# Softmax denominators of a hybrid encoder layer: laid out by VectorE and DRAM in place of TensorE and on-chip transfers

## The chip, the cores and the metric

The kernel runs on one core of a Trainium2 chip. A core has a matrix engine (TensorE, PE in the profile), a vector engine (VectorE, DVE), a scalar engine (ScalarE, ACT), a general engine (GpSimd, POOL) and a queue engine (SyncE, SP). Each works through its own list of instructions in order and waits at semaphores for the others. Transfers are issued from the SP and POOL queues and are carried out by 16 DMA engines. The metric is the device time of one execution in microseconds (us); lower is better. Three runs of the kernel before gave 528.19 to 529.47 us, median 529.1 us.

## What is computed

One layer of an encoder over 512 positions of width 1024, in float32: RMSNorm, one input projection, a recurrent group (a convolution and two linear scans) beside an attention group, an output projection, and a feed-forward part of width 4096 with a last RMSNorm. The change lies in the attention group, which has eight heads of width 64:

```
logits = einsum('bqhd,bqjhd->bhqj', qb, kg) * scale + bias          # per dilated window
lse    = logsumexp(logits);  p = exp(logits - lse)
o      = sum over the three windows of softmax(lse) * (p @ v)
```

The three windows with their softmax over `lse` are the same as one softmax over all keys, in which a key that lies in several windows counts several times. The kernel computes it so: exponentials e of all keys (the log of the multiplicity is in the bias), their row sum z for each query and head, and y = (e @ v) / z. The row sums are produced with one value per partition, because the queries lie on the partitions there. The product e @ v is produced transposed, with the 64 values of a head on the partitions and the 512 queries along the row, so 1/z has to be turned from a column into a row and repeated on 64 partitions. That turning is what is changed.

## The kernel before

Matrix products are done as three passes on numbers split into a high and a low part (`mm3`, lines 311 to 314). The weights come in blocks of 128x1024 into a ring of three buffers (`wraw`) by `emit_dma` (L230), are split by ACT (`conv_hi`, L247) and DVE (`conv_lo`, L269), and are used by PE some steps later.

The attention is worked in pairs of heads, p = 0 to 3, in a loop over i = 0 to 4 and u = 0 to 3 (lines 1142 to 1177). PE, ACT, DVE, POOL and, inside this loop, SP execute in the order in which the code writes their instructions out. A step (i, u) holds:

- `att_s(i, u)`: scores of pair i for one block of 128 queries, four matmuls (L797) into two PSUM banks. The tag `gs` has two banks, so the scores of the next step need that both banks were read.
- `att_t`: for pair i-1, transposes of the exponentials on PE (L838), copied out of PSUM by ACT (L843). `att_c` turns remaining 32-column pieces on DVE (L851).
- `att_e(i, u)`: DVE adds the bias tile `tw` to the scores and takes the row's least value (L813), ACT takes the exponential and its row sum (L814). The sums of a pair are eight columns in `zs[p]`.
- at u = 0, `att_z(i-1)`: the reciprocal of the eight sums (L868), and a copy that repeats each 16 times (L870), 128x128 in `z16`.
- `att_t` of the second head at u = 1 also transposes `z16` on PE (L840), and ACT copies the result back (L845). Row 32*qt + 16*e + w then holds the 128 values of query block qt and head e of the pair.
- at u = 1, `att_zd(i-1)`: four transfers on SP's queue (L877) copy each group of 32 rows, each row four times, into 128 partitions of `zrow`.
- `att_av`: the products e @ v (L941), of pair 0 at i = 2, of pairs 1 and 2 at i = 4, of pair 3 behind the loop. Each ends with `yp` = product * `zrow` on DVE (L947). From `yp` follow the squares for the attention's norm (`ysq`, L594 and L600), their column sums on PE (`turned`, L430, at 180.50 us) and the scaled `at` (L961).
- between them fillers: projections of the later pairs (`pqk`) and of the output (`pwo`), whose PSUM banks are emptied by DVE (L985), with `x` loaded by SP (L1049) in the same step as the weight sums `ws` (L1052).

The bias tiles `tw` are read from DRAM by pairs of SP transfers (L466, L468), at u = 2 for the first half and at u = 0 for the second half of a pair's query blocks. Each SP transfer also waits for the completion of the transfer issued eight before it, because there are eight completion semaphores in turn.

## Time and profile before

| what | us |
|---|---|
| median of three runs | 529.1 (528.19 to 529.47) |
| the profiled execution, its own time | 528.82 |
| its span, first to last instruction | 527.0 |
| PE busy | 520.1 |
| DVE busy | 433.7 |
| ACT busy | 357.1 |
| POOL busy | 65.8 |
| attention loop, first scores to the last product's `yp` | 95.3 to 177.8 |

The profile names a line of the program, its engine, output <- input, and a count. In a list of pieces in order of time the first number is the start from the span's start, the second the duration. In a row of a transfer the duration is that of the issue on the queue; the time from issue to landing stands apart. The 'DMA share' of a stretch is the mean busy share of the 16 DMA engines; values over 1 arise where packets of two queues overlap on an engine.

### The profile page before, as it was taken

The page shows a single profiled execution, that of the slowest core. Times are in us where ns is not written, and L with a number is a line of the kernel's source. Part 1 is how long each engine was busy: PE and PEld are TensorE (multiplying, and loading weights), DVE is VectorE, ACT ScalarE, POOL GpSimd, SP SyncE. Part 2 cuts the span into 40 slices and gives each one's busy share as a digit, 9 for nine tenths or more (in the row PEclk, how much of TensorE's full clock was granted, in tenths as well). Part 3 has the DMA queues.
Part 4 walks back from the last instruction along what each step waited for, and adds up shares of the span by engine and source line. Part 5 has one row for each costly group of instructions (what it writes and reads, how often), then busy time and mean ns, then how long its engine had stood idle before and what let it go on. Part 6 is the DMA issues. An engine that isn't in the chain of part 4 may idle for free.

```text
span 527.0 us, 8246 instructions
## 1 busy us (share of the span) xinstructions
PE 520.1 (99%) x3001; PEld 448.8 (85%) x3001; DVE 433.7 (82%) x665; ACT 357.1 (68%) x578; POOL 65.8 (12%) x88
## 2 busy tenths in 40 slices
PE   9999999999999999999999999999999999999995
PEld 8856888887887788899999888888999999888884
DVE  5898788997877888898779987889756987987885
ACT  6578983788856757585577755576467677655664
POOL 0184000000000131001300311001101200131000
PEclk9999999999999999999999999999999999999999
DMA  7646446596696498947495899976978497799704
GB/s 285 213 133 162 151 140 189 149 249 190 134 317 208 136 189 230 340 158 203 115 224 142 219 270 274 311 283 160 279 224 217 107 224 214 160 297 265 174 1 159
DMA packets 42441, 106.64 MB, mean 202 GB/s; under 512 B 4865, under 2 KB 15233, under 8 KB 42401
## 3 DMA queue, kind: packets, MB, share of 16 engines
q1 hardware_dynamic: 34848, 80.14, 45.9%
q0 software_dynamic: 7408, 25.79, 26.4%
q8 instruction: 23, 0.38, 0.3%
q10 hardware_dynamic: 144, 0.20, 0.1%
q14 instruction: 18, 0.14, 0.1%
HBM read 94.54 MB, written 4.23 MB: 187 GB/s over the span
## 4 chain that ended last, share of the span: by engine, by line
PE 98%; DVE 0%; issue 0%; DVEq 0%; ACT 0%; ACTq 0%
PE pu L313 10%; PE pu L312 10%; PE pu L314 10%; PE pd L312 10%; PE pd L314 10%; PE pd L313 10%; PE pqk L312 3%; PE pqk L314 3%; PE pqk L313 3%; PE pwo L312 3%; PE pwo L314 3%; PE pwo L313 3%; PE ps L797 2%; PE pav L941 2%; PE pt L838 2%; PE pv L312 2%
## 5 line engine op out<-in xcount | busy, mean ns | idle before, releaser
L269 DVE TENSOR_TENSOR wlo<-wraw,whi 128x1024 fp32r<-128x1024 f32 x71 | 86.6, 1220 | 23.8 <-ACT whi L247 23.5
L247 ACT ACTIVATE whi<-wraw 128x1024 fp32r<-128x1024 f32 x67 | 70.9, 1059 | 32.1 <-PE pd L314 20.2
L313 PE MATMUL pd<-wlo,ah 128*128 128x512 f32 (+1 forms) x195 | 75.2, 386 | 0.0
L312 PE MATMUL pd<-whi,ah 128*128 128x512 f32 (+1 forms) x195 | 75.2, 386 | 0.0
L314 PE MATMUL pd<-whi,al 128*128 128x512 f32 (+1 forms) x195 | 75.2, 386 | 0.0
L247 ACT ACTIVATE whi<-tw 128x1024 fp32r<-128x1024 f32 x38 | 40.2, 1060 | 40.5 <-DMA tw<-in_w_up_dram 12.2
L313 PE MATMUL pu<-hl,whi 128*128 128x256 f32 x224 | 63.4, 283 | 0.0
L314 PE MATMUL pu<-hh,wlo 128*128 128x256 f32 x224 | 63.4, 283 | 0.0
L312 PE MATMUL pu<-hh,whi 128*128 128x256 f32 x224 | 63.4, 283 | 0.0
L269 DVE TENSOR_TENSOR wlo<-tw,whi 128x1024 fp32r<-128x1024 f32 x38 | 46.4, 1220 | 18.6 <-ACT whi L247 18.6
L312 PE MATMUL pu<-h2h,whi 128*128 128x256 f32 (+1 forms) x200 | 60.1, 300 | 0.0
L314 PE MATMUL pu<-h2h,wlo 128*128 128x256 f32 (+1 forms) x200 | 60.0, 300 | 0.0
L313 PE MATMUL pu<-h2l,whi 128*128 128x256 f32 (+1 forms) x200 | 60.0, 300 | 0.0
L312 PEld LDWEIGHTS pu<-hh,whi 128*128 128x128 f32 x224 | 43.0, 192 | 0.0
L313 PEld LDWEIGHTS pu<-hl,whi 128*128 128x128 f32 x224 | 43.0, 192 | 0.0
L314 PEld LDWEIGHTS pu<-hh,wlo 128*128 128x128 f32 x224 | 43.0, 192 | 0.0
L314 PEld LDWEIGHTS pd<-whi,al 128*128 128x128 f32 x195 | 36.6, 188 | 7.4
L313 PEld LDWEIGHTS pd<-wlo,ah 128*128 128x128 f32 x195 | 36.6, 188 | 7.4
L312 PEld LDWEIGHTS pd<-whi,ah 128*128 128x128 f32 x195 | 36.6, 188 | 7.2
L247 ACT ACTIVATE whi<-ts 128x1024 fp32r<-128x1024 f32 x24 | 25.5, 1061 | 24.4 <-PE pd L314 18.1
L312 PEld LDWEIGHTS pu<-h2h,whi 128*128 128x128 f32 x200 | 38.3, 191 | 1.3
L314 PEld LDWEIGHTS pu<-h2h,wlo 128*128 128x128 f32 x200 | 38.3, 191 | 1.3
(276 smaller groups left out, 1246.0 us busy)
## 6 DMA issues: line engine op xcount, KB each, us to landing
wraw<-in_w_up_dram SPq DMA_DIRECT2D x25, 512.0 KB, 4.3
ts<-in_w_dn_dram POOLq DMA_DIRECT2D x24, 512.0 KB, 13.7
wraw<-in_w_dn_dram SPq DMA_DIRECT2D x24, 512.0 KB, 9.1
tw<-in_w_up_dram SPq DMA_DIRECT2D x15, 512.0 KB, 6.7
tw<-in_w_up_dram POOLq DMA_DIRECT2D x15, 512.0 KB, 8.3
wraw<-in_w_in_dram SPq DMA_DIRECT2D x13, 512.0 KB, 3.7
ts<-in_w_dn_dram SPq DMA_DIRECT2D x8, 512.0 KB, 7.1
tw<-in_w_dn_dram SPq DMA_DIRECT2D x8, 512.0 KB, 6.6
```

The lines of the kernel that those rows point to most:

```text
L247: act(hi, raws[i], AF.Copy)
L269: nc.vector.tensor_tensor(lo, r, f(splits[i][0]), op=OP.subtract)
L312: nc.tensor.matmul(o, lhsT=a[0], rhs=b[0], start=bool(first), stop=False, skip_group_check=on)
L313: nc.tensor.matmul(o, lhsT=a[0], rhs=b[1], start=False, stop=False, skip_group_check=on)
L314: nc.tensor.matmul(o, lhsT=a[1], rhs=b[0], start=False, stop=bool(last), skip_group_check=on)
L797: nc.tensor.matmul(psq[p][e][:, :NK], lhsT=sp[p, 0, n, e][:, c0:c0 + P], rhs=k, start=i == 0, stop=i == 1)
L838: nc.tensor.transpose(pt[:, i * P:(i + 1) * P], en[h][qt][:, k:k + P], ident)
L941: nc.tensor.matmul(pav[p][a, co], lhsT=vs[:, jt, h * DH:(h + 1) * DH], rhs=et[h, jt][:, ci], start=jt == 0 and i == 0, stop=jt == 3 and i ...
```

## The change

- The eight sums are ordered by head and then query block (column 4*e + qt in place of 2*qt + e).
- `att_z` writes their reciprocals into the first eight columns of a 128x32 tile that was zeroed once at the start (`rz32`, one more memset on POOL), and turns the tile on DVE in squares of 32x32 into `zt`. One transfer writes `zt` to a DRAM tile `zd`: all 32 rows of each square, 128 pieces of 32 values. It is issued by SP where `att_z` stands, at u = 0.
- `att_zd` reads `zrow` from there in one transfer: two rows of 512 values, each repeated on 64 partitions. It stands at u = 2 in place of u = 1, except for the last pair, where it stays at u = 1.
- Gone are the copy to 128x128, the PE transpose, ACT's copy out of PSUM, and the four transfers.

```diff
+    rz32 = consts.tile([P, 32], FT, name="rz32")
     nc.gpsimd.memset(mhalf, -0.5)
+    nc.gpsimd.memset(rz32, 0.0)
...
-            act(x, x, AF.Exp, scale=-1.0, bias=mn, accum_out=zs[p][:, 2 * qt + e:2 * qt + e + 1])
+            act(x, x, AF.Exp, scale=-1.0, bias=mn, accum_out=zs[p][:, 4 * e + qt:4 * e + qt + 1])
...
-        z = z16[h // 2] if (h % 2, jt) == (0, 1) else None
...
-        if z is not None:
-            nc.tensor.transpose(pt[:, 3 * P:], z, ident)
...
-        if z is not None:
-            act(z, pt[:, 3 * P:], AF.Copy)
...
+    zd = dram.tile([4, 32, P], FT, name="zd")
+
     def att_z(p):
-        rz = small("rz", 8)
-        nc.vector.reciprocal(rz, zs.pop(p))
-        z16[p] = g_("z16")[:, :P]
-        nc.vector.tensor_copy(z16[p], fan(rz, 0, 8, 16))
+        nc.vector.reciprocal(rz32[:, :8], zs.pop(p))
+        zt = work.tile([P, 32], FT, name="zt", tag="zt", bufs=2)
+        nc.vector.transpose(zt, rz32)
+        nc.sync.dma_start(bass.AP(tensor=zd.tensor, offset=zd.offset + 32 * P * p, ap=[[32, 4], [P, 32], [1, 32]]), zt)
 
     def att_zd(p):
         zrow[p] = g_("zrow")
-        t = z16.pop(p)
-        for qt in range(4):
-            r = t[32 * qt:32 * qt + 32]
-            nc.sync.dma_start(zrow[p][:, qt * P:(qt + 1) * P],
-                              bass.AP(tensor=r.tensor, offset=r.offset, ap=[r.ap[0], [0, 4], [1, P]]))
+        nc.sync.dma_start(zrow[p], bass.AP(tensor=zd.tensor, offset=zd.offset + 32 * P * p, ap=[[S, 2], [0, DH], [1, S]]))
...
-                if u == 1 and i >= 1:
+                if u == (1 if i == 4 else 2) and i >= 1:
                     att_zd(i - 1)
```

More of the change, by code (lines that the diff above doesn't have):

```diff
@@ L828, in blocks @@
         return (own + oth, slice(0, NK)) if hj else (oth + own, slice(S - NK, S))
-    z16 = {}
     def att_t(h, jt):
```

## The prediction

> **What bounds the kernel now.** I read the page's busy times first, then the chain that ended last, then PE's waits.

> ```profile
> span 527.0 us, 8246 instructions
> ...
> PE 520.1 (99%) x3001; PEld 448.8 (85%) x3001; DVE 433.7 (82%) x665; ACT 357.1 (68%) x578; POOL 65.8 (12%) x88
> ...
> PE 98%; DVE 0%; issue 0%; DVEq 0%; ACT 0%; ACTq 0%
> ```
> ```profile
> PE pwarm L142 <- PEq L1800: 0.8, 1, 0.8
> ```

> PE is busy in 99% of the span and makes 98% of the chain; its only recorded wait is 0.8 us before the first matmul. So an instruction taken from DVE, ACT, POOL or SP is worth nothing by itself, one taken from PE is worth its own time, and every new wait of PE is paid in full, because PE has no idle time in which to make it up. What can happen is therefore a small certain gain, and a loss where the new path to `zrow` makes something late that PE uses.

> How near to late things are is seen where the change lies. The chain in order of time, then DVE's list in order of time:

> ```profile
> 150.69 0.33 PE pt L838 x3
> 151.02 0.11 PE pt L840
> 151.13 0.33 PE pt L838 x3
> ...
> 153.53 0.56 PE ps L797 x3
> ```
> ```profile
> 130.46 0.69 DVE L947 TENSOR_TENSOR yp<-pav,zrow 128x512 f32<-128x512 f32 x1 [0.42 <-PE pav L941]
> ...
> 149.94 0.75 DVE L985 SCALAR_TENSOR_TENSOR x<-pwo,rcol,x 128x512 f32<-128x512 f32 x1 [0.71 <-DMA x<-in_xn_dram]
> ...
> 151.74 0.58 DVE L813 CUSTOM_DVE_ANT_0 e<-ps,tw 128x416 f32<-128x416 f32 x1
> ...
> 164.46 0.16 DVE L868 RECIPROCAL rz<-zz 128x8 f32<-128x8 f32 x1
> 164.65 0.23 DVE L870 COPY z<-rz 128x128 f32<-128x128 f32 x1
> ...
> 167.71 0.69 DVE L947 TENSOR_TENSOR yp<-pav,zrow 128x512 f32<-128x512 f32 x1 [2.14 <-PE pav L941]
> ...
> 177.10 0.69 DVE L947 TENSOR_TENSOR yp<-pav,zrow 128x512 f32<-128x512 f32 x1
> ...
> 179.42 0.69 DVE L600 TENSOR_TENSOR ysq<-ysq 128x512 f32<-128x512 f32 x1
> ```
> ```profile
> 180.50 0.60 PE L430 MATMUL pcs<-ident,ysq 128*128 128x128 f32 x4
> ```

> Two places are tight. At 149.94 DVE has already waited 0.71 us for a load of `x`; behind it stand the two L813 that empty the score banks, the first done at 151.74 + 0.58 = 152.32, and PE writes into that bank at 153.53: 1.2 us of slack. And the last pair's `yp` at 177.10 leads over `ysq`, done at 179.42 + 0.69 = 180.11, to PE's column sums at 180.50: 0.4 us.

> **What goes and what comes on the engines.** PE loses four transposes L840, 0.11 us each on the chain: -0.44 us, the one sure term. ACT loses four copies out of PSUM and DVE exchanges its copy for a turn of 128x32, whose nearest row is L851, the same operation on the same shape:

> ```profile
> L845 ACT ACTIVATE z<-pt x4: 263/270/273, 115.5 to 169.4; 128x128 f32<-128x128 f32 x4
> ```
> ```profile
> L851 DVE STREAM_TRANSPOSE ett<-e x32: 167/186/208, 111.6 to 173.5; 128x32 f32<-128x32 f32 x32
> ```

> 4 x 0.27 us of ACT and 4 x (0.23 - 0.19) us of DVE are saved, beside PE: counted as nothing. The order of the sums in `zs` costs nothing. The added memset on POOL stands behind one of 0.10 us and ahead of a wait for the first load:

> ```profile
> 1.25 0.10 POOL L136 MEMSET mhalf<- 128x4 f32 x1
> 3.56 0.19 POOL L337 COPY ag<-tw 128x8 f32<-128x8 f32 x1 [2.21 <-DMA tw<-in_xw_dram]
> ```

> Between nothing and twice that row's time (32 columns in place of 4), an estimate, it vanishes in those 2.21 us of waiting; without that wait it would delay the first matmuls by as much.

> **What goes and comes on SP's queue.** Sixteen transfers of 64 KB become four writes of 16 KB and four reads of 256 KB.

> ```profile
> L877 SPq DMA_DIRECT2D zrow<-z x16: 550/598/1107, 117.5 to 171.9; - x16
> ...
> DMA to landing us min/median/max: 2.1/2.1/6.6
> ```
> ```profile
> 122.26 0.43 SPq L468 DMA_DIRECT2D tw<-nbd  x1
> ...
> 137.48 2.54 SPq L877 DMA_DIRECT2D zrow<-z  x4
> 140.06 0.59 SPq L466 DMA_DIRECT2D tw<-nbd  x1
> ...
> 142.23 0.41 SPq L1052 DMA_DIRECT2D ws<-in_w_out_dram  x1
> 142.74 2.08 SPq L1049 DMA_DIRECT2D x<-in_xn_dram  x2
> ...
> 159.35 0.43 SPq L230 DMA_DIRECT2D wraw<-in_w_up_dram  x1
> ```

> Issue time falls, from four times 0.6 us to twice 0.6 us per pair. The write waits for DVE's turn (for the last pair 164.65 + 0.19 = 164.84) and holds what is queued behind it: for pairs 0 to 2 the q transfers or loads of `x`, by no more than its own 0.6 us, because the turn is done when SP comes there; for pair 3, where it comes last, the first block of `w_up`, issued at 159.35 before, which goes to 165.5. ACT first touches that block at 194.13, so 6 us later is covered; if it weren't, ACT's split of it and PE's use would move with it.

> ```profile
> 194.13 1.05 ACT L247 ACTIVATE whi<-wraw 128x1024 fp32r<-128x1024 f32 x1
> ```

> POOL's transfers keep their place. The write's landing is needed by the read alone. For pairs 0 to 2 the bias tiles stand between them; for pair 3 only that block, so SP waits there for the landing, with later weight blocks behind it, which are as early as that first one.

> **The unknown: how long the read holds its DMA engines.** The read names two rows and repeats each 64 times. The least leading count in any transfer of the trace is 32, so how a count of 2 is dealt out is shown nowhere. The bounds come from the rate of one engine and from two loads of the same 256 KB, one plain, one that repeats a row on 128 partitions:

> ```profile
> q1 hardware_dynamic: 34848, 80.14, 45.9%
> ```
> ```profile
> L1049 SPq DMA_DIRECT2D x<-in_xn_dram x8: 328/334/1656, 142.7 to 159.0; - x8
> ...
> DMA to landing us min/median/max: 3.5/5.3/7.4
> ```
> ```profile
> L1719 SPq DMA_DIRECT2D fgt<-in_fg_dram x2: 481/640/798, 466.8 to 469.8; - x2
> ...
> DMA to landing us min/median/max: 10.0/12.0/14.0
> ```

> 80.14 MB in 45.9% of 16 x 527 us is 20.7 KB per us and engine. Spread on 16 engines the 262 KB hold each for 0.8 us, as the four old transfers did; on two for 6.3 us, 5.5 us more. One engine alone, 12.7 us, is the far end. The repeating load lands 12.0 - 5.3 = 6.7 us later than the plain one at the median. The value nearest to that is 5.5 us, and I take two engines; the queue was full around `fgt` too, so this is a choice and not a proof.

> [...]

> **What lies behind the read.** A transfer has its share on every engine, so what follows on the queue waits for those two.

> ```profile
> 137.50:145.00 7.50, 7.50 (x42) 6.55 (x41) 6.12 (x18) 6.78 (x17) 0.00 (x0) 1.00 0.61 119
> 145.00:165.00 20.00, 20.00 (x119) 16.23 (x119) 16.24 (x42) 12.58 (x33) 0.00 (x0) 1.00 0.97 316
> 165.00:167.50 2.50, 2.50 (x24) 1.41 (x20) 0.57 (x1) 1.24 (x2) 0.00 (x0) 1.00 0.49 195
> 167.50:172.50 5.00, 5.00 (x34) 4.27 (x32) 4.39 (x11) 3.11 (x9) 0.00 (x0) 1.00 0.15 35
> ```

> The last two columns are DMA share and GB/s.

> Pair 0's read stands behind the bias load that was issued at 122.26, so it is issued by 122.7 at the latest; at 2.1 + 5.5 us it lands by 130.3, and its `yp` starts at 130.46 because the products end then: hidden, though barely (each us of lateness would first use up DVE's 0.42 us of idle time). Pair 1's read stands ahead of `ws` and `x`. The engines are idle for 0.39 x 7.5 = 2.9 us in 137.5 to 145, which takes up that much; 5.5 - 2.9 = 2.6 us remain. `x` then comes at 152.5 in place of 149.94, the first L813 ends at 154.9, and PE, which arrives at 153.53 - 0.33 = 153.2, waits 1.7 us.

> Pair 2's read falls where the share is 0.97, so nothing takes it up. Its own `yp` comes at 167.71 and is safe, but both reads together, 11.0 - 2.9 - 0.6 = 7.5 us, push the end of the backlog from 165 + 0.49 x 2.5 = 166.2 to 173.7. The last pair's write, issued at 165, lands at the end of that backlog, and only then may the read start: 173.7 + 2.1 (least landing of `zrow`) + 5.5 = 181.3. `yp` would have come at 177.10 + 1.7 - 0.44 = 178.4; it is 2.9 us late, of which 0.4 are slack: PE waits 2.5 us at L430. Sum: -0.44 + 1.7 + 2.5 = +3.8 us.

> With one engine at the 316 GB/s and 0.97 of the full stretch (20.4 KB per us) this is unchanged; if a lone pair of engines is a tenth faster, the read adds 5.0 us, the two waits are 1.2 and 1.5 us, and the sum is +2.3 us. I take +3.0 us between them. On the profiled execution's 528.82 us that is 531.8; the median of the runs is 0.3 us above it, so I forecast 532.1.

> **The rivals.**
> (a) Not slower: the read is spread widely. From four engines up it holds them 3.2 us, 2.4 more than before, less than the 2.9 us gap, and both places stay covered. Then only the transposes go: 528.7. For it: every transfer in the trace runs on many engines, SP's issue time falls, and the DMA share of 0.15 after 167.5 leaves the last pair 5 us. Against it: the landing of `fgt`.
> (b) The last read lands like `fgt`: 12.0 us after an issue at 173.2, at 185.2, against 178.1: 7.1 - 0.4 = 6.7 us at L430, with 1.5 at L797 and -0.44 in all +7.8: 536.9. Against it: the queue is emptier there.
> (c) Two engines, but the waits shorter than 1 us each, because the loads behind are issued ahead of need: 529.1 to 530.7. Against it: DVE's 0.71 us at L985, already a wait for such a load.

> **Chances and range.** The measurement tells 0.3%, 1.6 us, from no change. Two engines with more than that: 0.50; like `fgt`: 0.10; (c) 0.08; (a) 0.29; faster by over 0.3%, for which no row gives a mechanism beyond 0.44 us, 0.03. Slower 0.60, same 0.37, faster 0.03. The likeliest case alone lies between 530.7 and 535; the range takes in (a) below, with the run to run spread, and (b) above: 528.4 to 537.

> **What the new profile would show.** The transposes: no L840, PE's busy time down 0.44. The read: landing of `zrow` at 7 us or more against 2 to 5 if it is spread. Stage by stage: an L985 that waits for `x` over 0.71 us near 150, PE waits on DVE at L797 near 153; `yp` of the last pair waiting on `zrow` and PE on L600 at L430. If PE still has no wait, (a) holds and the forecast is wrong. It is wrong as well if the lateness shows at loads that I took as covered, such as the bias tiles.

## The result, and the profile after

The changed kernel takes 536.04 us (535.63 to 536.71) where the kernel before takes 529.17 us (528.19 to 529.47): the ratio is 1.0134, 95% interval 1.0116 to 1.0152. It is slower, by 6.9 us. The profiled execution took 535.63 us.

The page after: span, busy times and, last, the chain that ended last by engine.

```profile
span 533.9 us, 8221 instructions
...
PE 521.4 (98%) x2997; PEld 448.5 (84%) x2997; DVE 433.5 (81%) x665; ACT 356.0 (67%) x574; POOL 65.8 (12%) x89
...
PE 86%; DMA 9%; DVE 2%; ACT 1%; issue 1%; SPq 0%; DVEq 0%; ACTq 0%
```

PE has four matmuls fewer, yet the span is 6.9 us longer. Before, 98% of the chain was PE; now 9% of it is DMA. PE's waits (total, times, longest) were one of 0.8 us; now there are three more, all behind DVE:

```profile
PE ps L799 <- DVE mn L815: 2.6, 1, 2.6
PE pcs L432 <- DVE ysq L602: 1.5, 1, 1.5
PE pt L837 <- DVE cs L437: 1.2, 1, 1.2
PE pwarm L144 <- PEq L1793: 0.8, 1, 0.8
```

DVE's own list in order of time shows what it waited for: pair 0's `zrow` near 132, the loads of `x` near 154 and the last pair's `zrow` near 184. (L940 was L947, L978 was L985, L799 was L797, L837 was L838, L432 was L430.)

```profile
132.10 0.69 DVE L940 TENSOR_TENSOR yp<-pav,zrow 128x512 f32<-128x512 f32 x1 [2.73 <-DMA zrow<-zd]
...
154.21 0.75 DVE L978 SCALAR_TENSOR_TENSOR x<-pwo,rcol,x 128x512 f32<-128x512 f32 x1 [5.07 <-DMA x<-in_xn_dram]
...
184.12 0.69 DVE L940 TENSOR_TENSOR yp<-pav,zrow 128x512 f32<-128x512 f32 x1 [2.08 <-DMA zrow<-zd]
```

The last `yp` is at 184.12 where it was at 177.10: 7.0 us later, of which 0.4 us were slack. The chain in order of time shows the way there: pair 3's write takes 5.0 us to land, and its read 9.0 us.

```profile
170.02 4.96 DMA zd<-zt
174.98 0.02 SPq L871
175.05 8.98 DMA zrow<-zd
```

And there is a loss that no list of waits shows. Behind the longest wait the granted clock (third column from the right) falls to half; the last two columns are DMA share and GB/s (the share of 1.01 is queue q1's alone, 101.4%, so a value over 1 needs no second queue):

```profile
157.50:160.00 2.50, 2.50 (x11) 2.18 (x10) 2.10 (x4) 1.64 (x5) 0.00 (x0) 0.50 0.88 152
160.00:162.50 2.50, 2.50 (x11) 2.08 (x10) 1.64 (x5) 1.19 (x4) 0.00 (x0) 0.83 1.01 390
```
```profile
156.65 0.45 PE L799 MATMUL ps<-kk,qh 128*128 128x416 f32 x1 [2.59 <-DVE mn L815]
...
161.99 0.35 PE L799 MATMUL ps<-kk,qh 128*128 128x416 f32 x1
```

From these scores to the next ones PE needs 161.99 - 156.65 = 5.34 us. In the kernel before the same work ran from 153.37 to 156.85:

```profile
153.37 0.35 PE L797 MATMUL ps<-kk,qh 128*128 128x416 f32 x1
...
156.85 0.35 PE L797 MATMUL ps<-kk,qh 128*128 128x416 f32 x1
```

That is 3.48 us, so 1.9 us are lost there. In this execution the loss adds up along PE as 1.2 + 2.6 + 1.9 + 1.5 - 0.4 (the transposes) = 6.8 us of the 6.9 us of span.

### The profile page after: what moved, and what is told of

It is laid out like the page before. It is cut to its first block, busy times and chain, and to the rows that moved or that the text cites. A ratio compares the mean times of both kernels' runs of the same rounds, so it can differ in the third digit from the quotient of the medians.

```text
span 533.9 us, 8221 instructions
## 1 busy us (share of the span) xinstructions
PE 521.4 (98%) x2997; PEld 448.5 (84%) x2997; DVE 433.5 (81%) x665; ACT 356.0 (67%) x574; POOL 65.8 (12%) x89
## 3 DMA queue, kind: packets, MB, share of 16 engines
q1 hardware_dynamic: 33592, 80.20, 45.9%
## 4 chain that ended last, share of the span: by engine, by line
PE 86%; DMA 9%; DVE 2%; ACT 1%; issue 1%; SPq 0%; DVEq 0%; ACTq 0%
PE pu L315 10%; PE pu L316 10%; PE pu L314 10%; PE pd L315 9%; PE pd L314 9%; PE pd L316 9%; DMA zrow<-zd 4%; DMA x<-in_xn_dram 3%; PE pqk L314 2%; PE pqk L315 2%; PE pqk L316 2%; DMA zd<-zt 2%; PE pv L314 2%; PE pg L516 1%; PE pv L315 1%; PE pp L316 1%
## 5 line engine op out<-in xcount | busy, mean ns | idle before, releaser
L315 PEld LDWEIGHTS pu<-h2l,whi 128*128 128x128 f32 x200 | 38.3, 191 | 1.3
```

The costliest lines, as they stand in the source:

```text
L315: nc.tensor.matmul(o, lhsT=a[0], rhs=b[1], start=False, stop=False, skip_group_check=on)
```

## The experiments

The theory to test: the read's leading count of 2 puts its 256 KB on two DMA engines, and what stands behind it comes late. The main rival: a read that repeats one row of DRAM, or the way through DRAM, is slow in any case. "Leading count" means the outermost count of the read's pattern that is not one. A read with a count of 2 is called narrow below, one with a larger count spread. All edits are to the changed kernel, and all times stand against 529.1 to 529.3 us of the kernel before on the same chip.

**Leading count 64 in place of 2.** The read is split by head, so that each half can begin with its 64 repeats:

```diff
-        nc.sync.dma_start(zrow[p], bass.AP(tensor=zd.tensor, offset=zd.offset + 32 * P * p, ap=[[S, 2], [0, DH], [1, S]]))
+        for e in range(2): nc.sync.dma_start(zrow[p][64 * e:64 * e + 64], bass.AP(tensor=zd.tensor, offset=zd.offset + 32 * P * p + S * e, ap=[[0, DH], [1, S]]))
```

> Each of the four reads is split by head into two transfers whose leading count is 64 instead of 2; bytes, place in the queue and everything else stay. Theory (few engines: a leading count of 2 puts the 256 KB on two DMA engines): zrow lands within 5 us of its issue for pairs 0 to 2, PE has no wait but the 0.8 us of pwarm, the granted clock stays above 0.95 after 157, and only the four transposes are left of the change: 528.7 us, between 528.2 and 529.3. Rival (repeating read: 64 or 128 reads of one row of DRAM are slow however they are dealt out, or the way through DRAM is): zrow still lands 10 us or more after its issue, the waits at L799, L837 and L432 stay, 535 to 537 us.

Measured: 528.18 us (527.37 to 528.38), ratio 0.9977 (0.9967 to 0.9987). All three waits are gone, and `zrow` lands after 6.0 us at the median, and after 2.9 us at the least, in the last pair:

```profile
PE 519.6 (99%) x2997; PEld 448.4 (85%) x2997; DVE 433.9 (82%) x665; ACT 356.8 (68%) x574; POOL 65.8 (12%) x89
```
```profile
DMA to landing us min/median/max: 2.9/6.0/6.2
```

The whole loss hangs on how the read is dealt out; the rival falls. The landing of 6.0 us missed the 5 us expected, which did no harm. This version is also faster than the kernel before, by 0.1 to 0.3%: the 0.5 us that PE's busy time lost (520.1 to 519.6) and as much again that no row explains.

**Two transfers, but a leading count of 2.** This separates the count from the splitting:

```diff
-        nc.sync.dma_start(zrow[p], bass.AP(tensor=zd.tensor, offset=zd.offset + 32 * P * p, ap=[[S, 2], [0, DH], [1, S]]))
+        for e in range(2): nc.sync.dma_start(zrow[p][64 * e:64 * e + 64], bass.AP(tensor=zd.tensor, offset=zd.offset + 32 * P * p + S * e, ap=[[0, 2], [0, 32], [1, S]]))
```

> The same two transfers per pair as in the wide version, but each with its 64 repeats written as 2 times 32, so that the leading count is 2. Theory (leading count): as the changed kernel, zrow 10 to 12 us after its issue, PE waits at L837 about 1.2, at L799 about 2.6, at L432 about 1.5 us: 535 to 537 us. Rival (what helps is that a pair's read comes as two transfers of 128 KB, or that the order of completions shifts by one): as the wide version, 528.2 to 529.3 us. In between, if two transfers are started on different engines: zrow lands after 5 to 8 us and 529.5 to 533 us.

Measured: 541.79 us (540.86 to 542.71), ratio 1.0235 (1.0216 to 1.0253). Splitting does not help, the count does; but it came out 5 us above the expectation. The three waits are longer. The clock falls at two of them, for 3.4 us from about 160, just behind the wait, and for 6.8 us from about 191, when the wait has a good microsecond to go. It does not fall at the wait of 2.6 us that ends at 137.68:

```profile
PE pcs L432 <- DVE ysq L602: 3.6, 1, 3.6
PE ps L799 <- DVE mn L815: 3.0, 1, 3.0
PE pt L837 <- DVE cs L437: 2.6, 1, 2.6
```
```profile
137.50:140.00 2.50, 2.32 (x12) 1.98 (x13) 2.44 (x10) 2.45 (x5) 1.04 (x1) 1.00 0.41 96
160.00:162.50 2.50, 2.50 (x10) 2.27 (x11) 2.26 (x4) 1.55 (x6) 0.00 (x0) 0.50 0.61 146
192.50:195.00 2.50, 2.50 (x9) 2.02 (x8) 2.31 (x5) 0.19 (x1) 0.66 (x1) 0.50 0.00 0
```

Why each wait grew by 0.4 to 2.1 us over the single transfer's was not tried.

**A leading count of 4.** As before, with `[[0, 4], [0, 16], [1, S]]`.

> All four reads as two transfers each, with the 64 repeats written as 4 times 16: a leading count of 4. Theory (the leading count is the number of engines): each engine is held half as long as with 2, 3.2 us per pair, zrow lands 5 to 9 us after its issue, PE waits less than 0.5 us anywhere and the clock stays at 1.00: 528.2 to 529 us. Rival (any leading count under 16 is dealt to two engines, or a transfer of this form is slow anyway): zrow lands after 10 us or more and the waits come back: 533 us or more.

Measured: 528.38 us (527.31 to 529.49), ratio 0.9982 (0.9968 to 0.9996), no wait of PE but `pwarm`'s. How many engines a read holds can be seen in stretches of a microsecond in which almost nothing else moves. The packets and the share of the 16 engines, first in the changed kernel (128.0 to 128.8), then with two transfers of count 2 (179.5 to 180.5), then with count 4 (170.0 to 170.8), then with count 64 (168.0 to 168.8):

```profile
DMA packets 21, 0.04 MB, mean 51 GB/s; under 512 B 1, under 2 KB 1, under 8 KB 21
...
q1 hardware_dynamic: 21, 0.04, 13.4%
```
```profile
q1 hardware_dynamic: 24, 0.05, 13.3%
```
```profile
q1 hardware_dynamic: 39, 0.08, 26.6%
```
```profile
q1 hardware_dynamic: 53, 0.09, 52.8%
```

**One read narrow at a time.** Pair 1 alone, pair 3 alone, all but pair 3 and all but pair 2 keep the one transfer with a count of 2; the other pairs read with a count of 64:

```diff
-        nc.sync.dma_start(zrow[p], bass.AP(tensor=zd.tensor, offset=zd.offset + 32 * P * p, ap=[[S, 2], [0, DH], [1, S]]))
+        for e in (range(2) if p != 1 else ()): nc.sync.dma_start(zrow[p][64 * e:64 * e + 64], bass.AP(tensor=zd.tensor, offset=zd.offset + 32 * P * p + S * e, ap=[[0, DH], [1, S]]))
+        if p == 1: nc.sync.dma_start(zrow[p], bass.AP(tensor=zd.tensor, offset=zd.offset + 32 * P * p, ap=[[S, 2], [0, DH], [1, S]]))
```

For pair 3 alone the two conditions are `p != 3` and `p == 3`, for all but pair 3 `p == 3` and `p != 3`, for all but pair 2 `p == 2` and `p != 2`.

> Only pair 1 keeps the one read with leading count 2; the reads of pairs 0, 2 and 3 are two transfers with leading count 64. Theory (each read delays what stands behind it by itself): PE waits at L799 for 2.6 us (2.1 to 3.1) because x lands late, the granted clock then is 0.50 for about 3.4 us, which costs 1.9 us, nothing at L837 and L432: 528.7 + 2.6 + 1.9 = 533.2 us (532.3 to 534). Rival (the three reads share one backlog, and without pair 0's the later ones find room): the wait at L799 is under 1 us and the clock does not fall: 528.7 to 530 us. Second rival (the clock falls for another reason than the wait): 2.6 us of wait and 531.3 us.

Measured: 532.19 us (530.96 to 533.18), ratio 1.0052 (1.0032 to 1.0072). One narrow read, ahead of the loads of `x`, is enough for the wait of 2.6 us at L799 and, in the profiled execution, for the low clock:

```profile
PE ps L799 <- DVE mn L815: 2.6, 1, 2.6
```
```profile
155.00:157.50 2.50, 2.14 (x7) 1.97 (x8) 2.50 (x8) 1.36 (x4) 0.00 (x0) 0.50 0.68 155
```

The median is 1 us under the expectation and just below its range; two later measurements of this kernel (below) gave 531.77 and 530.72 us.

> Only pair 3 keeps the read with leading count 2, the other reads are two transfers with leading count 64. Theory (pair 3's lateness is made by the backlog that the earlier narrow reads leave, which holds up its write): the write lands 2 to 3 us after its issue as in the wide version, the read is issued at about 167 and takes the 9 us that it took in the changed kernel, so it lands at 176 and yp, due at 176.5, does not wait: 528.2 us (527.5 to 529). Rival (the last read is too long in any case): it takes 11 to 12 us as the others did, lands at 178 to 179, PE waits 1 to 2 us at L432: 529.2 to 530.3 us.

Measured: 527.87 us (527.41 to 528.4), ratio 0.9978 (0.9968 to 0.9988), no wait at L432. The last read alone costs nothing: it is issued at 166.48, 8.6 us earlier than in the changed kernel, and `yp` does not wait.

```profile
166.48 0.57 SPq L872 DMA_DIRECT2D zrow<-zd  x1
```
```profile
176.21 0.69 DVE L941 TENSOR_TENSOR yp<-pav,zrow 128x512 f32<-128x512 f32 x1
```

> Pairs 0 to 2 keep the read with leading count 2, pair 3's read is two transfers with leading count 64. Theory (the times of the waits add up): PE waits 1.2 us at L837 and 2.6 us at L799, loses 1.9 us to the lower clock, and does not wait at L432, as the last read lands before 180 and yp is due only at about 182: 528.2 + 5.7 = 533.9 us (533 to 535). Rival (the end of the DMA backlog alone sets the time, and the last read counts for little): 535 to 536.5 us with a wait at L432 of more than 0.5 us.

Measured: 533.82 us (532.53 to 534.68), ratio 1.0098 (1.0077 to 1.0118), no wait at L432. So in the changed kernel pair 3's read is worth 536.04 - 533.82 = 2.2 us, although alone it is worth nothing. In the profiled execution, the fastest of these, the wait at L799 was 2.2 us and the clock did not fall.

> Pairs 0, 1 and 3 keep the read with leading count 2, pair 2's is two transfers with leading count 64. Theory (pair 2's read pushes the end of the backlog, and pair 3's write lands only there: 5.0 us after its issue in the changed kernel, 2.4 in the wide one): the write lands within 3 us, the last read ends by 182, no wait at L432 over 0.4 us, and the time is that of the version with pair 3 wide: 533.8 us (533 to 534.6). Rival (pair 1's read and the late loads of x alone make that backlog): the write still takes 4.5 us or more, PE waits 1 us or more at L432, 535 to 536.5 us.

Measured: 533.8 us (531.5 to 534.62), ratio 1.0068 (1.0047 to 1.0089), no wait at L432. With pair 2's read spread, pair 3's write (L867) lands within 2.0 us, where it took 5.0, and the narrow read that follows (L872) is in time:

```profile
170.79 0.58 SPq L867 DMA_DIRECT2D zd<-zt  x1
...
172.83 0.56 SPq L872 DMA_DIRECT2D zrow<-zd  x1
```

Behind the narrow reads of pairs 0 and 1, pairs 2 and 3 thus cost their 2.2 us only together: pair 2's read holds up pair 3's write, and pair 3's read is too long to make it good.

A narrow read also holds the queue that issues. In the changed kernel SP, at the eighth transfer behind pair 1's read, waits for that read to land, because the eight completion semaphores are used in turn; with a count of 64 SP issues the same load at 146.82, 0.05 us behind the issue before it:

```profile
SPq L470 <- DMA zrow<-zd: 4.8, 1, 4.8
```

Pair 2's write is issued at 154.85, where it was at 148.46 with a count of 64, and what follows it on the queue is later too. How much of the lateness of pairs 2 and 3 this makes was not tried.

**The reads where the four transfers stood.** All reads narrow, but one step earlier for pairs 0 to 2:

```diff
-                if u == (1 if i == 4 else 2) and i >= 1:
+                if u == 1 and i >= 1:
```

> The changed kernel with all its reads with leading count 2, but issued where the four transfers of the kernel before were, one step (u = 1 instead of 2) earlier for pairs 0 to 2, ahead of four bias loads. Theory (the narrow read is harmful by what stands behind it while the engines are full): pair 0's read is issued 2 to 3 us earlier and no longer late (1.2 us), pair 1's uses more of the idle engines before the loads of x (1 to 2.6 us and the clock's 1.9), pair 3's stays: 530 to 534 us. Rival (the bias loads behind the read are late instead): DVE waits for tw and PE for it at L799, 535.5 us or more.

Measured: 532.49 us (530.45 to 532.88), ratio 1.005 (1.0032 to 1.0068): at the median 3.5 us of the loss come from the place, not from the two engines alone. In the profiled execution pair 1's read is issued at 138.06 instead of 140.71, the loads of `x` are back in time, with 0.70 us of waiting as in the kernel before, and the clock stays at 1.00:

```profile
138.06 0.57 SPq L871 DMA_DIRECT2D zrow<-zd  x1
```
```profile
150.48 0.75 DVE L978 SCALAR_TENSOR_TENSOR x<-pwo,rcol,x 128x512 f32<-128x512 f32 x1 [0.70 <-DMA x<-in_xn_dram]
```

Three waits of PE of 0.8, 0.7 and 0.6 us are left. The bias loads behind the reads made DVE wait 0.41 and 0.46 us; the second of these stands where the kernel before waited 0.60 us for such a load, so the rival's mechanism shows in the first alone, at a small size. The profiled execution is the fastest of the four, 530.45 us. The others took 532.23 to 532.88 us, and one of them had a mean granted clock of 0.994, so what is read here of the loads of `x` and of the clock need not hold for them.

**Matmuls of ones in PE's wait.** Does the fall of the clock cost time in the end? Ten (or five) matmuls of ones (the trace counts each of them twice), into columns of PSUM that nobody reads, stand ahead of the scores at which PE waits:

```diff
-    QSEQ = (0, 3, 1, 2)
+    QSEQ, lastpt = (0, 3, 1, 2), {}
...
-        c0 = P * qt
+        c0 = P * qt; [nc.tensor.matmul(lastpt[0][:, 3 * P:], lhsT=one, rhs=one, start=True, stop=True) for _ in range(10 * ((p, u) == (3, 2)))]
...
-        pt = ps_("pt", "et")
+        pt = lastpt[0] = ps_("pt", "et")
```

> The changed kernel, and ten 128x128 matmuls of ones, into columns that nobody reads, just ahead of the scores at which PE waits 2.6 us in pair 3. Theory (the granted clock falls because PE is idle that long): PE's wait there falls under 0.8 us, the granted clock stays above 0.9 from 157 to 161, and about 1.9 us come back: 534.1 us (533.6 to 534.7). Rival (the clock falls for another reason): it is 0.50 there again and the time is 536 us; if the matmuls take longer than the wait, above 536.

Measured: 535.8 us (533.96 to 536.43), ratio 1.0116 (1.0092 to 1.014). The clock stays at 1.00, but the expected 1.9 us do not come: PE now waits 2.4 us at L432 in place of 1.5, and twice 0.5 at L799, and the last `yp` is at 183.91, 0.2 us earlier than without the matmuls.

```profile
PE pcs L432 <- DVE ysq L602: 2.4, 1, 2.4
PE pt L837 <- DVE cs L437: 1.0, 1, 1.0
PE ps L799 <- DVE mn L815: 1.0, 2, 0.5
```
```profile
157.50:160.00 2.50, 2.50 (x16) 2.15 (x15) 1.92 (x4) 1.68 (x5) 0.00 (x0) 1.00 0.65 189
```

What PE gains ahead of pair 3's read it waits for at that read. The four executions of the changed kernel say the same. A fall to 0.50 for 3.41 us takes 0.003 off the mean granted clock of an execution, and the mean is on record for each: 0.996 in the profiled one, with its fall, and 0.993, 0.997 and 0.998 in the others. Two of these, 0.997 and 0.998, are too high for a fall, as the kernel before never has more than 0.999 without one; they took 535.73 and 536.35 us, the other two 535.63 and 536.71 us. So as far as four executions tell, the 1.9 us are a term of one execution's sum, and the time of the changed kernel does not hang on them.

> As the version with pairs 0 to 2 narrow and pair 3 wide, with the ten matmuls of ones ahead of the scores at which PE waits 2.6 us. In the filled version of the changed kernel the clock stayed at 1.00 but the wait at L432 grew from 1.5 to 2.4 us; here the last read can't take the gain. Theory (the low clock costs 1.9 us of its own): no clock of 0.5, no wait at L432, 533.9 - 1.9 + 0.4 (a second short wait at L799) = 532.4 us (531.8 to 533). Rival (the low clock costs nothing, the work behind it makes it up): 533.5 us or more.

Measured: 533.35 us (532.96 to 534.12), ratio 1.0085 (1.0065 to 1.0103), beside 533.82 without the matmuls: no difference that can be told. The clock stayed at 1.00, but it had done so in the unfilled profile as well, and pair 0's wait was 1.9 us here and 1.4 there.

The same with pair 1 alone narrow, where no later read is in the way:

> The version with pair 1 alone narrow once more, beside the next one, as its four times lay between 530.96 and 533.18: 532.2 us (531.6 to 533).

> The version with pair 1 alone narrow, with the ten matmuls of ones ahead of the scores at which PE waits 2.6 us; no later read can take the gain here. Theory (the low granted clock behind the wait costs up to 1.9 us): no clock of 0.50, a wait of about 0.5 us left, 530.3 to 531.3 us, and the single times lie closer together. Rival (the clock costs nothing in the end): 532 us or more.

Measured: 531.77 us (529.85 to 532.92) without and 531.41 us (529.88 to 532.39) with ten matmuls; ratios 1.0038 (1.0025 to 1.0051) and 1.0036 (1.0025 to 1.0047). The ten take 2.4 us, longer than the wait of 2.0 us, so they can hide their gain. Hence five:

> Pair 1 alone narrow, with five matmuls of ones (1.2 us) ahead of the scores instead of ten (2.4 us), so that they end inside the wait of 2.0 to 2.6 us and cost nothing themselves. Theory (the low granted clock behind the wait costs up to 1.9 us in the end): the wait left is 0.8 to 1.4 us, the clock stays at 1.00, and the median lies 0.8 to 1.9 us below the version without them in this call. Rival (it costs nothing in the end): both medians within 0.4 us.

> Pair 1 alone narrow, without the matmuls of ones, for comparison in the same call: 531.8 to 532.2 us, as in its two earlier runs, and a granted clock of 0.50 for 3.4 us behind the wait.

Measured: 530.75 us (530.11 to 532.08) with five and 530.72 us (529.36 to 532.87) without; ratios 1.0026 (1.0011 to 1.004) and 1.0026 (1.0009 to 1.0044). In the profiles the unfilled kernel has a wait of 2.0 us and the clock at 0.50, the filled one a wait of 0.8 us and 1.00. At the median the rival holds: filling the wait gains nothing that can be measured. But the unfilled kernel's twelve times fall into two groups, six from 529.36 to 530.26 and six from 531.18 to 532.87, while nine of the filled kernel's twelve lie together from 530.11 to 530.86. The mean granted clock tells the groups apart: it is 0.993 to 0.995 in the six long executions and 0.996 to 0.999 in the six short ones, and the kernel before has 0.996 to 0.999 in all its 23 runs beside them. The measurement with ten matmuls shows the same of its unfilled kernel: 0.993 to 0.995 in the six executions from 531.92 to 532.92 us, 0.997 to 0.999 in the six from 529.85 to 531.62 us. None of the 24 executions with matmuls is under 0.996.

So the clock falls in only some executions of the unfilled kernel, these are longer by 2.5 and 1.7 us on average, and, as far as this mean tells, the matmuls prevent the fall. Their medians, 530.75 and 531.41 us, lie between the averages of the two groups, 529.8 and 532.3 us for five matmuls and 530.7 and 532.4 us for ten, as if the matmuls cost something in the executions that would not have had a fall. Whether the long executions are long by the clock alone or had a longer wait as well stays open, because only one execution of each kernel is profiled. The first four executions of this kernel are too few to show it: there 532.83 us came at a mean clock of 0.999.

## Why the prediction was right in direction and wrong in size

- **Two engines for a count of 2: right.** The prediction's two were an estimate from the landing of `fgt`; no row of the kernel before shows them for this read. The runs show 13.4% of 16 engines, 2.1, and 528.2 us as soon as the count is 64. That a plain load has its share on most engines shows in the kernel before: from 33.5 to 34.2 us a block of `wraw` alone takes 83.7% of 16 engines, 13.4. The rate was too low: alone the two move 51 GB/s, 25.5 KB per us and engine, where 20.7 were taken, so a read that meets nothing else holds them for 5.1 us and not for 6.3. Rival (a), a read spread widely, gave 528.7 us; that is what the kernel with counts of 4 and 64 does.
- **The transposes, -0.44 us: right.** PE's busy time falls by 0.5 us in the kernel with a count of 64. The edits on ACT, DVE and POOL cost nothing that shows.
- **Pair 0 "hidden, though barely": wrong by 1.2 us.** The read was given the least landing time of `zrow`, 2.1 us, plus 5.5. It stands behind the bias loads, and even when spread it takes 6.0 us at the median there. 121.00 to 132.10 is 11.1 us, about 6.0 + 5.1.

```profile
121.00 0.60 SPq L871 DMA_DIRECT2D zrow<-zd  x1
...
140.71 0.59 SPq L871 DMA_DIRECT2D zrow<-zd  x1
```

- **Pair 1, 1.7 us: the place right, the size 2.6.** What failed here is the gap of 2.9 us that was to take up as much of the read. One step later, and behind pair 0's wait, the transfer was issued at 140.71, 3.2 us after the first of the old four (137.48). In the kernel before, the DMA share from 137.5 to 140.7 is 0.60, so 0.40 x 3.2 = 1.3 of the 2.9 us lay ahead of the read. `x` came 4.3 us late (154.21 for 149.94) instead of 2.6. Issued at 138.06, the same read made no such delay in the execution that was profiled.
- **The clock: not in the prediction.** 1.9 us in the profiled execution, behind the wait just named; with the matmuls of ones ahead of these scores the clock stayed at 1.00. In the four executions of the changed kernel the time does not hang on it.
- **Pair 3, 2.5 us at L432: the mechanism right, shown by undoing pair 2's read alone; the size differs.** The landing was put at 181.3 and came at 175.05 + 8.98 = 184.0. Of these 2.7 us, 1.3 lie in the end of the backlog (173.7 forecast, 175.05 measured) and 1.4 in the read itself (7.6 forecast, 9.0 measured). The 2.1 + 5.5 left out that three weight blocks follow on the same queue. In the trace the read's packets go at about 25 per us and 84 ns each up to 180, and at 11 to 18 per us and about 130 ns from then on, with the blocks' packets beside them. That the blocks cause it is not shown: some of their packets run beside the read before 180 as well. The wait itself is only 1.5 us, because PE comes there late already.
- **The sum: the landing of the last pair's read is the step that failed.** The prediction added the waits, -0.44 + 1.7 + 2.5 = 3.8 us, and took 3.0 between this and 2.3; 6.9 came. In that sum the last landing sets the end (181.3 - 177.1 - 0.4 = 3.8), and the kernel with the wait filled bears this out: time regained ahead of the landing is lost again there. The landing was put at 181.3 us and came at 184.0, and these 2.7 us make 6.5 of the 3.8. The 0.8 us taken off for a faster pair of engines came to nothing: alone the pair was faster, but in its place on the queue the read took longer. Two terms were too small: the backlog ahead of the read, for which the gap of 2.9 us was counted in full, by 1.3 us, and the read itself by 1.4 us. The terms ahead of that landing were too small as well, but they count only where it does not bind. With pair 3's read spread, 533.82 - 529.09 = 4.7 us remain, where the prediction's terms give -0.44 + 1.7 = 1.3; missing there are the wait for pair 0's `zrow`, 1.4 us in that profile, and the rest of pair 1's wait.
- **Rival (b), 536.9 us, came nearest by luck.** It had the last read landing at 185.2, but its 12 us of landing were 9.0, its start was 1.8 us too early, and its wait of 6.7 us at L430 was 1.5.

## What to carry to other kernels

Write a repeating read so that the outermost count of its pattern is large, or split it into parts whose outermost count is large: here, with the same bytes in the same place of the queue, a count of 2 cost 6.9 us and counts of 4 and 64 gained 0.7 to 1.0 us. When a transfer holds few engines, follow everything behind it on the queue to its user, and take its base time from the queue's backlog at that place, not from the least landing in the trace (2.1 us for `zrow` before; 6.0 us at the median with a count of 64). A gap in the DMA share is worth only what lies behind the moment of issue: 1.3 of the 2.9 us lay ahead of it. And count what stands behind a long transfer on its issuing queue by completion semaphores too: here SP stood still for 4.8 us.

## What the runs showed of the hardware that was not expected

Waits of PE at L799 of 2.6 us in the changed kernel, of 3.0 us with two narrow transfers, and of 2.6, 2.0 and 2.0 us in the three profiles with pair 1 alone narrow were followed by a granted clock of 0.50 for 3.4 us (from 157.42 to 160.83 in the changed kernel). At one of 3.6 us, at L432 with two narrow transfers, the clock fell for 6.83 us, from 1.1 us before the wait's end. Three times a wait of this size brought no fall: 2.6 us at L837 in the kernel with two narrow transfers, 2.4 us at L432 in the one with ten matmuls, and 2.2 us at L799 with pair 3's read spread. Waits of 1.9 us and less never brought one, those of 1.9, 1.4 and 1.2 us at L837 among them. In the record of the granted clock of the changed kernel the stretches at full speed ahead of and behind the fall are 153.60 and 372.05 us, 45 and 109 times the fall's 3.413 us; in that of the kernel before the one stretch at full speed is 518.83 us, 152 times. What decides whether a wait of this size brings a fall, no run shows.
